# A three-pass fp32 feed-forward whose split weight sums are stored by the first token group and loaded by the other two

## The chip, the cores and the metric

The kernel runs on one core of one Trainium2 chip. A core has TensorE (PE in the profile), VectorE (DVE), ScalarE (ACT), GpSimd (POOL), and SyncE (SP), which in this kernel issues nearly all DMA transfers; each engine executes its own instruction list in order. The metric is the device time of one execution in microseconds (us). The kernel before takes 2158.03 us, the median of three runs (2157.86 to 2159.79).

## The reference

One layer of a decoder in fp32, over 2048 prompt tokens and 8 sample tokens, model width 1024, feed-forward width 2816:

```python
def _layer(x, ...):
    xn = _rmsnorm(x, norm1_g)
    z = jnp.einsum('btd,de->bte', xn, w_in)        # [xr | gr | q | k | v]
    ...                                            # RG-LRU group, windowed attention group
    mix = jnp.concatenate([_rmsnorm(rec, rec_norm_g), _rmsnorm(att, attn_norm_g)], axis=-1)
    h = x + jnp.einsum('bte,ed->btd', mix, w_out)
    hn = _rmsnorm(h, norm2_g)
    ff = jax.nn.silu(jnp.einsum('btd,df->btf', hn, w_gate)) * jnp.einsum('btd,df->btf', hn, w_up)
    y = h + jnp.einsum('btf,fd->btd', ff, w_down)
    return y, new_k, new_v, new_conv, h_last
```

A last RMSNorm gives the outputs; the caches and recurrent states are outputs too.

## The kernel before

**Two phases.** Phase A (to about 706 us) computes the norm, the input projection, the RG-LRU and attention groups and the output projection, for four sub-sequences of some 512 tokens. The residual stream h goes to the DRAM tensor `hs`. Phase B is the feed-forward. It goes over three token groups (0, 1, 2), each of two halves of 344 or 342 columns, and in each group over 11 pairs of 128-row chunks of the feed-forward width.

**Three passes per product.** A matrix product in fp32 is made of three passes of a reduced-precision format (fp32r): each operand is split into a high part (the cast) and a low part (value minus cast), and TensorE adds high x high, high x low and low x high.

**Seven products per pair.** Gate and up are computed by a scheme of the Strassen kind (Winograd's variant): a 2 x 2 block product needs seven block products in place of eight, of sums of weight blocks and sums of token blocks. So per pair and matrix TensorE does 7 products of 12 matmuls, in the order `PRODS = [1, 2, 6, 7, 5, 3, 4]`, and then 96 plain matmuls for down. In its list g of pair p, down of pair p-1 and u of pair p follow each other.

**Weights.** `mixed_weights` (L995 of the kernel before) loads the four raw blocks of a pair and matrix, 256 KB each, from SyncE (L1000), and forms the sums S5, S6, S7 (`combine`, L1006; on GpSimd) and S3 (on VectorE). `keep_weights` then makes the split tile of each of the seven: the cast on ScalarE (L990) and the subtraction on GpSimd for products at even places of `PRODS`, on VectorE for odd ones (L991). A split tile is 512 KB, both parts side by side. `down_weights` (L1022) does the same without sums, all low parts on GpSimd. There are 7 buffers for raw blocks and 8 for split tiles. The same work is done in each of the three groups, from the same weights.

**Results.** `products` adds the seven PSUM results into c_g and c_u on VectorE (L1057), applies silu on ScalarE (L1048), multiplies (L1051), and splits the product into fh (cast, L1053) and fl (subtraction, L1054). `down` multiplies them (L1107 to L1109) and adds into y (L1111, VectorE). `finish` does the last norm and stores `out_yT` from SyncE (L1138); `y_load` (L986) reloads h into the buffers that come free.

**Tokens.** `hn_mix` reloads h from `hs` (n<-hs, L320), scales it (L324), forms the sums of token blocks (L332) and stores them in `mixed` (L328); `hn_load` loads them and splits them (L379 to L381).

**Order.** Every piece of work is a generator that yields due times (`Chains`); the due time becomes the priority of the instructions made next. A scheduler that simulates a timeline takes these priorities and fixes the order of each engine's list. So a change of due times or a removed instruction moves others. An engine that waits for a semaphore holds everything behind it in its list, SyncE's transfers included.

**The last sub-sequence.** While `out_half` finishes the last sub-sequence, ScalarE squares each of the eight chunks of h (L245, L248) and GpSimd adds seven of them into `hacc` (L249). `last_norm`, due at T_H3 = T_B0 + 25, makes the norm's factors of it.

## Time and profile before

| what | value |
|---|---|
| median of three runs | 2158.03 us (2157.86 to 2159.79) |
| the profiled execution | 2159.32 us, span 2157.5 us |
| TensorE busy | 2064.9 us (96%) |
| VectorE busy | 1504.3 us (70%) |
| ScalarE busy | 937.9 us (43%) |
| GpSimd busy | 1167.4 us (54%) |
| DMA | 300.73 MB, mean 139 GB/s |

"Busy" of TensorE includes modelled ends, so a full row doesn't mean peak speed. The trace gives for each instruction its start, its duration and, in brackets, the idle time before it and what ended it ("<-ACT w_g L990": it waited for the cast of line 990). Line numbers are those of the kernel before; in the kernel after, lines behind the first part of the diff have other numbers.

### The profile page before, as it was taken

To read this page: it belongs to the slowest core of one execution; us is meant where nothing else is said; L and a number is where in the kernel's file an instruction comes from. 1 tells how busy PE (TensorE), PEld (TensorE's weight loads), DVE (VectorE), ACT (ScalarE), POOL (GpSimd) and SP (SyncE) were. 2 spreads that over 40 slices of the span, in tenths; PEclk is the share of its full clock that TensorE was granted. 3 is DMA by queue.
4 is the path that set the end of the run, shared out by engine and by line. 5 is a ranking of instruction groups with operands and counts; after the bars stand their busy time and mean duration, and the time that the engine had idled before them with its cause. 6 is when DMAs were issued, how large, how long until landed. Compare 5 with 4: busy or idle time off the path is not lost.

```text
span 2157.5 us, 34673 instructions
## 1 busy us (share of the span) xinstructions
PE 2064.9 (96%) x12454; PEld 1950.7 (90%) x12454; DVE 1504.3 (70%) x2683; ACT 937.9 (43%) x1890; POOL 1167.4 (54%) x968
## 2 busy tenths in 40 slices
PE   8999899999999899999998999999998999999997
PEld 8887687878777799999998999999998999999997
DVE  6757974766985867766657867666758875565566
ACT  5746763563553533333334433333334433333332
POOL 5211342020122786676577866776677766765763
PEclk9999899999999999999999999999999999999999
DMA  8764384575677533333225242333225242222221
GB/s 304 244 211 137 126 295 152 176 256 192 208 248 268 165 108 97 100 111 109 92 73 175 81 158 90 100 123 105 93 75 168 87 136 74 84 79 74 69 79 53
DMA packets 155563, 300.73 MB, mean 139 GB/s; under 512 B 19424, under 2 KB 60784, under 8 KB 155376
## 3 DMA queue, kind: packets, MB, share of 16 engines
q1 hardware_dynamic: 152192, 296.00, 42.1%
q10 hardware_dynamic: 3200, 2.51, 0.4%
...
HBM read 243.62 MB, written 55.90 MB: 139 GB/s over the span
## 4 chain that ended last, share of the span: by engine, by line
PE 68%; DVE 12%; DMA 7%; POOL 4%; ACT 4%; issue 4%; SPq 1%; DVEq 0%; ACTq 0%; POOLq 0%
PE pd L1108 6%; PE pd L1109 6%; PE pd L1107 6%; PE ps_u L1067 6%; PE ps_u L1069 6%; PE ps_u L1068 6%; PE ps_g L1067 5%; PE ps_g L1069 5%; PE ps_g L1068 5%; PE ip L232 3%; PE ip L233 3%; PE ip L234 3%; DMA n<-hs 2%; PE op L233 1%; PE op L234 1%
## 5 line engine op out<-in xcount | busy, mean ns | idle before, releaser
L1107 PE MATMUL pd<-fh,w_d 128*128 128x342 f32 (+1 forms) x1056 | 339.4, 323 | 12.2 <-DVE y L1111 6.6
L1108 PE MATMUL pd<-fl,w_d 128*128 128x342 f32 (+1 forms) x1056 | 340.7, 323 | 9.7 <-DVE fl L1054 9.7
L1109 PE MATMUL pd<-fh,w_d 128*128 128x342 f32 (+1 forms) x1056 | 340.4, 323 | 0.0
L1067 PE MATMUL ps_g<-hn,w_g 128*128 128x342 f32 (+1 forms) x924 | 296.0, 321 | 7.8 <-ACT w_g L990 6.1
L1111 DVE TENSOR_TENSOR y<-y,pd 128x342 f32<-128x342 f32 (+1 forms) x528 | 249.5, 503 | 71.5 <-PE pd L1109 68.8
L1067 PE MATMUL ps_u<-hn,w_u 128*128 128x342 f32 (+1 forms) x924 | 295.4, 320 | 1.9 <-DVE y L1111 1.6
L1069 PE MATMUL ps_g<-hn,w_g 128*128 128x342 f32 (+1 forms) x924 | 296.0, 320 | 0.0
L1068 PE MATMUL ps_g<-hn,w_g 128*128 128x342 f32 (+1 forms) x924 | 295.8, 320 | 0.0
L1068 PE MATMUL ps_u<-hn,w_u 128*128 128x342 f32 (+1 forms) x924 | 295.0, 319 | 0.0
L1069 PE MATMUL ps_u<-hn,w_u 128*128 128x342 f32 (+1 forms) x924 | 294.9, 320 | 0.0
L1107 PEld LDWEIGHTS pd<-fh,w_d 128*128 128x128 f32 x1056 | 200.2, 190 | 16.9 <-DVE y L1111 8.0
L232 PE MATMUL ip<-xn,w_in 128*128 128x512 f32 (+1 forms) x560 | 199.6, 364 | 13.2 <-ACT xn L237 9.2
L1108 PEld LDWEIGHTS pd<-fl,w_d 128*128 128x128 f32 x1056 | 201.8, 191 | 10.4 <-DVE fl L1054 10.4
L233 PE MATMUL ip<-xn,w_in 128*128 128x512 f32 (+1 forms) x560 | 201.6, 364 | 0.5 <-DVE xn L238 0.5
L1109 PEld LDWEIGHTS pd<-fh,w_d 128*128 128x128 f32 x1056 | 201.8, 191 | 0.0
L234 PE MATMUL ip<-xn,w_in 128*128 128x512 f32 (+1 forms) x560 | 199.0, 358 | 0.2 <-POOL w_in L223 0.2
L991 POOL TENSOR_TENSOR w_d<-rd,w_d 128x512 fp32r<-128x512 f32 x132 | 182.9, 1396 | 1.5 <-ACT w_d L990 1.3
L1067 PEld LDWEIGHTS ps_g<-hn,w_g 128*128 128x128 f32 x924 | 174.8, 189 | 8.4 <-ACT w_g L990 6.4
L991 POOL TENSOR_TENSOR w_u<-ru,w_u 128x512 fp32r<-128x512 f32 x66 | 98.7, 1495 | 152.5 <-ACT w_u L990 152.5
L1057 DVE TENSOR_TENSOR c_u<-c_u,ps_u 128x342 f32<-128x342 f32 (+1 forms) x231 | 114.3, 507 | 92.4 <-PE ps_u L1069 90.8
L1067 PEld LDWEIGHTS ps_u<-hn,w_u 128*128 128x128 f32 x924 | 174.1, 188 | 2.7 <-ACT w_g L990 1.4
L1069 PEld LDWEIGHTS ps_g<-hn,w_g 128*128 128x128 f32 x924 | 174.8, 189 | 0.2 <-DVE w_g L991 0.2
...
## 6 DMA issues: line engine op xcount, KB each, us to landing
w_in<-split_w SPq DMA_DIRECT2D x84, 512.0 KB, 3.5
...
w_out<-split_w SPq DMA_DIRECT2D x48, 512.0 KB, 5.0
split_w<-w_in SPq DMA_DIRECT2D x28, 512.0 KB, 5.1
...
```

What stands on the lines that cost most here:

```text
L232: nc.tensor.matmul(out, wh, xh, start=first, stop=False)
L233: nc.tensor.matmul(out, wh, xl, start=False, stop=False)
L234: nc.tensor.matmul(out, wl, xh, start=False, stop=last)
L991: lo_eng.tensor_tensor(w[:, 1, :], src, w[:, 0, :].bitcast(F32), op=ALU.subtract)
L1057: nc.vector.tensor_tensor(o, a, b, op)
L1067: nc.tensor.matmul(ps, wh, hi, start=kk == 0, stop=False)
L1068: nc.tensor.matmul(ps, wh, lo, start=False, stop=False)
L1069: nc.tensor.matmul(ps, wl, hi, start=False, stop=kk == 3)
L1107: nc.tensor.matmul(ps, w[:, 0, c:c + P], hi, start=h == 0, stop=False)
L1108: nc.tensor.matmul(ps, w[:, 0, c:c + P], lo, start=False, stop=False)
L1109: nc.tensor.matmul(ps, w[:, 1, c:c + P], hi, start=False, stop=h == 1)
L1111: nc.vector.tensor_tensor(ys[gi, n, m], ys[gi, n, m], ps, ALU.add)
```

## The change

In group 0, the split tiles of products 6, 7, 5 and 3 are also stored, each 512 KB, from SyncE to a DRAM tensor for gate or up (L_ST = 5 before the product's due time; 2 after it for the first pair). In groups 1 and 2 these four tiles are loaded from there (L_SS = 11 before the product's due time), the raw block A21 is not loaded, and its sums, casts and subtractions are not made. Products 1, 2 and 4 are split as before in every group.

The squares of the last sub-sequence no longer are made in `out_half`. `last_norm` reloads the eight chunks from `hs` (SyncE), due from T_B0 + 38 in steps of 4, squares them on ScalarE, adds them on GpSimd, and makes the norm's factors 6 after the last.

```diff
@@ -41,6 +41,7 @@
 DVE_MUL = 2
 N_EARLY = 3
 T_FS = 12.0
+L_SS, L_ST = 11.0, 5.0
 D_TB = 0.0
 U_M = 1.76
 U_G, U_D = 7 * U_M, 14.1
@@ -49,7 +50,7 @@
 T_OP = [187.9747, 327.9525, 449.1331, 501.2336]
 T_OPA, L_LM = 539.4805, 52.6622
 T_B0 = 586.0461
-T_H3 = T_B0 + 25
+T_H3, D_H3 = T_B0 + 38, 4.0
 T_B = [T_B0 + i * (NPAIR * U_P + D_TB) for i in range(3)]
 O_KF = [8, 9, 10, 11, 12, 13, 0, 4, 1, 5, 2, 6, 3, 7]
 O_KL = [0, 4, 1, 5, 2, 6, 3, 7, 8, 9, 10, 11, 12, 13]
@@ -195,6 +196,7 @@
         rs2 = cp.tile([P, 4, 5], F32, name="rs2")
         hs = dp.tile([P, KD, NTOK], F32, name="hs")
         mixed = dp.tile([3, 7, P, 4, TP], F32, name="mixed")
+        split_s = {x: dp.tile([NPAIR, 4, P, 2, 512], F32, name=f"split_{x}") for x in "gu"}
         split_w = dp.tile([22, 2, P, 2, 512], F32, name="split_w")
 
         warm = cp.tile([P, 1], F32, name="warm")
@@ -885,13 +887,7 @@
                 with ahead(L_EV):
                     nc.vector.tensor_tensor(ps[:, :T], ps[:, :T], state[s]["late"][:, :T], ALU.mult)
                     nc.vector.tensor_tensor(xs[:, :T], xs[:, :T], ps[:, :T], ALU.add)
-                yield t + 3, ("hq", s, m - 1)
-                if m == 0:
-                    state[s]["hacc"] = accp.tile([P, TM], F32, tag="acc", name=f"hacc{s}")
-                acc = state[s]["hacc"]
-                add_square(acc, xs[:, :T], T, m == 0, f"h{s}_{m}")
                 nc.scalar.dma_start(hs[:, m, c0:c0 + T], xs[:, :T])
-                fire(("hq", s, m))
 
             def fin_a():
                 yield (T_OP[2], ("h", 3, 3), ("xr", 3, 3), ("h", 3, 2), ("h", 3, 1), ("h", 3, 0))
@@ -991,11 +987,17 @@
                 lo_eng.tensor_tensor(w[:, 1, :], src, w[:, 0, :].bitcast(F32), op=ALU.subtract)
                 ws[key] = w
                 fire(key)
+                return w
+
+            SPLIT = (6, 7, 5, 3)
 
             def mixed_weights(src, gi, p, x):
                 yield t_prod(gi, p, x, 0) - 18
                 A = {}
                 for h, q in ((0, 0), (0, 1), (1, 0), (1, 1)):
+                    if gi and (h, q) == (1, 0):
+                        A[h, q] = None
+                        continue
                     A[h, q] = raw_tile(f"r{x}{gi}_{p}_{h}{q}")
                     nc.sync.dma_start(A[h, q], src[2 * p + h][:, q * 512:q * 512 + 512])
                 A11, A12, A21, A22 = A[0, 0], A[0, 1], A[1, 0], A[1, 1]
@@ -1008,16 +1010,27 @@
 
                 S = {1: A11, 2: A12, 4: A22}
                 for i, r in enumerate(PRODS):
-                    yield t_prod(gi, p, x, i) - 9
+                    tr = t_prod(gi, p, x, i)
+                    if gi and r in SPLIT:
+                        yield tr - L_SS
+                        w = whl_tile(f"w_{x}{gi}_{p}_{r}")
+                        nc.sync.dma_start(w.bitcast(F32), split_s[x][p, SPLIT.index(r)])
+                        ws[x, gi, p, r] = w
+                        fire((x, gi, p, r))
+                        continue
+                    yield tr - 9
                     if r == 6:
                         S[5] = combine(A21, A22, ALU.add, 1)
                         S[6] = combine(S[5], A11, ALU.subtract, 2)
-                        yield t_prod(gi, p, x, i) - 8
+                        yield tr - 8
                     if r == 7:
                         S[7] = combine(A11, A21, ALU.subtract, 3)
                     if r == 3:
                         S[3] = combine(A12, S[6], ALU.subtract, 4)
-                    keep_weights((x, gi, p, r), f"{x}{gi}_{p}_{r}", S[r], nc.gpsimd if i in LO_POOL else nc.vector)
+                    w = keep_weights((x, gi, p, r), f"{x}{gi}_{p}_{r}", S[r], nc.gpsimd if i in LO_POOL else nc.vector)
+                    if r in SPLIT:
+                        with at(tr - L_ST if p else tr + 2):
+                            nc.sync.dma_start(split_s[x][p, SPLIT.index(r)], w.bitcast(F32))
 
             def down_weights(gi, p, t):
                 for i, (q, h) in enumerate(((0, 0), (0, 1), (1, 0), (1, 1))):
@@ -1138,9 +1151,20 @@
                     nc.sync.dma_start(yT[:, m, o:o + nn], v)
 
             def last_norm(s):
-                _, T, _, w, nt = SUBS[s]
-                yield T_H3
-                rstd_cols(state[s]["hacc"][:, :T], w, nt, 0, rs2[:w, s, :nt], f"h{s}", 0, True)
+                c0, T, _, w, nt = SUBS[s]
+                for m in range(KD):
+                    yield T_H3 + D_H3 * m
+                    if m == 0:
+                        acc = accp.tile([P, TM], F32, tag="acc", name=f"hacc{s}")
+                    x = stage(f"h{s}_{m}")[:, :T]
+                    keep(nc.sync.dma_start(x, hs[:, m, c0:c0 + T]))
+                    if m == 0:
+                        nc.scalar.square(acc[:, :T], x)
+                    else:
+                        nc.scalar.square(x, x)
+                        nc.gpsimd.tensor_tensor(acc[:, :T], acc[:, :T], x, op=ALU.add)
+                yield T_H3 + D_H3 * KD + 6
+                rstd_cols(acc[:, :T], w, nt, 0, rs2[:w, s, :nt], f"h{s}", 0, True)
                 fire(("h", s))
 
             ch.add(last_norm(3))
```

The instruction lists of before and after differ at many places; three of them matter below. In the names, `w_g_0_6` is the split gate tile of pair 0 and product 6, `s_g_0` a sum of gate blocks of pair 0, `rg_4_00` a raw block, `fl_10_10` a low part of pair 10; the number behind the last underscore is that of the allocation.

GpSimd, passage from phase A to phase B; before:

```order
L991 TENSOR_TENSOR w_g_0_5_7763<-s_g_0_7751,w_g_0_5_7763 128x512
L991 TENSOR_TENSOR w_g_0_6_7755<-s_g_0_7753,w_g_0_6_7755 128x512
L249 TENSOR_TENSOR hacc_6969<-hacc_6969,sq_h_1_6989 128x512
L249 TENSOR_TENSOR hacc_6969<-hacc_6969,sq_h_2_7010 128x512
L249 TENSOR_TENSOR hacc_6969<-hacc_6969,sq_h_3_7031 128x512
L249 TENSOR_TENSOR hacc_6969<-hacc_6969,sq_h_4_7050 128x512
L249 TENSOR_TENSOR hacc_6969<-hacc_6969,sq_h_5_7069 128x512
L249 TENSOR_TENSOR hacc_6969<-hacc_6969,sq_h_6_7088 128x512
L249 TENSOR_TENSOR hacc_6969<-hacc_6969,sq_h_7_7094 128x512
L1006 TENSOR_TENSOR s_g_0_7758<-rg_0_00_7664,rg_0_10_7668 128x512
L991 TENSOR_TENSOR w_g_0_4_7785<-rg_0_11_7670,w_g_0_4_7785 128x512
```

and now:

```order
L987 TENSOR_TENSOR w_g_0_1_7716<-rg_0_00_7643,w_g_0_1_7716 128x512
L1008 TENSOR_TENSOR s_g_0_7738<-rg_0_00_7643,rg_0_10_7647 128x512
L1008 TENSOR_TENSOR s_g_0_7730<-rg_0_10_7647,rg_0_11_7649 128x512
L1008 TENSOR_TENSOR s_g_0_7732<-s_g_0_7730,rg_0_00_7643 128x512
L987 TENSOR_TENSOR w_g_0_5_7744<-s_g_0_7730,w_g_0_5_7744 128x512
L987 TENSOR_TENSOR w_g_0_6_7734<-s_g_0_7732,w_g_0_6_7734 128x512
L1008 TENSOR_TENSOR s_u_0_7828<-ru_0_10_7726,ru_0_11_7728 128x512
L987 TENSOR_TENSOR w_u_0_1_7786<-ru_0_00_7722,w_u_0_1_7786 128x512
L1008 TENSOR_TENSOR s_u_0_7830<-s_u_0_7828,ru_0_00_7722 128x512
L1008 TENSOR_TENSOR s_u_0_7852<-ru_0_00_7722,ru_0_10_7726 128x512
```

The seven adds are gone from here, the third gate sum stands first, and the sums for the up matrix follow directly.

VectorE, end of group 0 (pair 10) and beginning of group 1 (pair 0); before:

```order
L381 TENSOR_TENSOR hn_1_4_12588<-hn_1_4_12588 128x342
L1051 TENSOR_TENSOR c_u_10_10_7300<-c_u_10_10_7300,c_g_10_10_7288 128x344
L991 TENSOR_TENSOR w_g_0_7_12756<-s_g_0_12754,w_g_0_7_12756 128x512
L1054 TENSOR_TENSOR fl_10_01_7295<-c_u_10_01_7299,fh_10_01_7291 128x344
L381 TENSOR_TENSOR hn_1_5_12609<-hn_1_5_12609 128x342
L381 TENSOR_TENSOR hn_1_7_12620<-hn_1_7_12620,hn_1_6_12616 128x342
L1057 TENSOR_TENSOR c_g_0_00_7302<-c_g_0_01_7303,ps_g_0_2_12657 128x342
L1054 TENSOR_TENSOR fl_10_10_7296<-c_u_10_10_7300,fh_10_10_7292 128x344
```

and now:

```order
L1070 TENSOR_TENSOR c_u_10_10_7279<-c_u_10_10_7279,ps_u_10_4_12684 128x344
L383 TENSOR_TENSOR hn_1_3_12673<-hn_1_3_12673,hn_1_2_12669 128x342
L1064 TENSOR_TENSOR c_u_10_10_7279<-c_u_10_10_7279,c_g_10_10_7267 128x344
L1067 TENSOR_TENSOR fl_10_01_7274<-c_u_10_01_7278,fh_10_01_7270 128x344
L383 TENSOR_TENSOR hn_1_4_12680<-hn_1_4_12680 128x342
L383 TENSOR_TENSOR hn_1_5_12701<-hn_1_5_12701 128x342
L1067 TENSOR_TENSOR fl_10_10_7275<-c_u_10_10_7279,fh_10_10_7271 128x344
L1070 TENSOR_TENSOR c_g_0_00_7281<-c_g_0_01_7282,ps_g_0_2_12749 128x342
```

The weight subtraction, one token split and the add into c_g no longer stand ahead of `fl_10_10`; `hn_1_4` now does.

TensorE at the same place, shortly ahead of that fl; before (ahead of these rows stand nine down matmuls of the first three outputs with the 00 parts):

```order
L1107 MATMUL pd_10_3_0_12722<-fh_10_00_7290,w_d_10_00_12555 128x344
L1108 MATMUL pd_10_3_0_12722<-fl_10_00_7294,w_d_10_00_12555 128x344
L1109 MATMUL pd_10_3_0_12722<-fh_10_00_7290,w_d_10_00_12555 128x344
L1107 MATMUL pd_10_4_0_12738<-fh_10_00_7290,w_d_10_01_12676 128x344
L1108 MATMUL pd_10_4_0_12738<-fl_10_00_7294,w_d_10_01_12676 128x344
L1107 MATMUL pd_10_0_0_12695<-fh_10_10_7292,w_d_10_10_12624 128x344
L1107 MATMUL pd_10_1_0_12703<-fh_10_10_7292,w_d_10_10_12624 128x344
L1107 MATMUL pd_10_2_0_12714<-fh_10_10_7292,w_d_10_10_12624 128x344
L1107 MATMUL pd_10_3_0_12722<-fh_10_10_7292,w_d_10_10_12624 128x344
L1108 MATMUL pd_10_0_0_12695<-fl_10_10_7296,w_d_10_10_12624 128x344
```

and now, from the first down matmul on:

```order
L1120 MATMUL pd_10_0_0_12787<-fh_10_00_7269,w_d_10_00_12647 128x344
L1121 MATMUL pd_10_0_0_12787<-fl_10_00_7273,w_d_10_00_12647 128x344
L1122 MATMUL pd_10_0_0_12787<-fh_10_00_7269,w_d_10_00_12647 128x344
L1120 MATMUL pd_10_0_0_12787<-fh_10_10_7271,w_d_10_10_12716 128x344
L1120 MATMUL pd_10_1_0_12795<-fh_10_00_7269,w_d_10_00_12647 128x344
L1121 MATMUL pd_10_1_0_12795<-fl_10_00_7273,w_d_10_00_12647 128x344
L1122 MATMUL pd_10_1_0_12795<-fh_10_00_7269,w_d_10_00_12647 128x344
L1121 MATMUL pd_10_0_0_12787<-fl_10_10_7275,w_d_10_10_12716 128x344
L1122 MATMUL pd_10_0_0_12787<-fh_10_10_7271,w_d_10_10_12716 128x344
```

The first matmul with `fl_10_10` was the 19th of the down matmuls and is now the 8th.

SyncE in a steady stretch of group 1, pairs 3 and 4; before:

```order
L1000 DMA rg_4_00_14336<-in_wgate 128x512
L1000 DMA rg_4_01_14338<-in_wgate 128x512
L1000 DMA rg_4_10_14340<-in_wgate 128x512
L1026 DMA rd_3_10_14595<-in_wdown 128x512
L1000 DMA rg_4_11_14342<-in_wgate 128x512
L320 DMA n_4_0_14426<-hs 128x342
L1026 DMA rd_3_00_14516<-in_wdown 128x512
L328 DMA mixed<-n_4_0_14426 128x342
L328 DMA mixed<-n_0_1_13837 128x342
L320 DMA n_1_1_14611<-hs 128x342
L1000 DMA ru_4_01_14651<-in_wup 128x512
L1026 DMA rd_3_01_14631<-in_wdown 128x512
```

and now:

```order
L1002 DMA rg_4_00_14339<-in_wgate 128x512
L1002 DMA rg_4_01_14341<-in_wgate 128x512
L1002 DMA rg_4_11_14343<-in_wgate 128x512
L1002 DMA ru_4_00_14622<-in_wup 128x512
L1039 DMA rd_3_00_14495<-in_wdown 128x512
L1039 DMA rd_3_10_14568<-in_wdown 128x512
L1017 DMA w_u_3_6_14319<-split_u 128x1024
L1017 DMA w_u_3_7_14337<-split_u 128x1024
L1017 DMA w_u_3_5_14361<-split_u 128x1024
L1017 DMA w_u_3_3_14379<-split_u 128x1024
L322 DMA n_4_0_14411<-hs 128x342
L330 DMA mixed<-n_4_0_14411 128x342
```

One raw load less stands there, and four loads of split up tiles stand behind the raw loads of the next pair.

## The prediction

> **What bounds the kernel now.** I read three views in this order: the windows by stage, the groups and waits of TensorE, and then, around each gap, the instructions in order of time. All times are microseconds of the profiled execution (span 2157.5, its own time 2159.32). The median of the three timed runs is 2158.03, so 1.3 is taken off at the end.
>
> ```profile
> 706.00:745.00 39.00, 29.77 (x170) 28.04 (x169) 36.46 (x44) 21.12 (x43) 31.40 (x22) 0.91 0.55 177
> 745.00:1150.00 405.00, 401.30 (x2544) 399.60 (x2544) 271.05 (x442) 146.18 (x279) 285.40 (x222) 1.00 0.31 100
> 1150.00:1320.00 170.00, 158.56 (x988) 156.14 (x987) 133.08 (x199) 70.43 (x147) 122.09 (x94) 0.96 0.40 129
> 1320.00:1640.00 320.00, 319.06 (x2024) 318.02 (x2023) 215.56 (x350) 113.38 (x215) 217.33 (x169) 1.00 0.31 98
> 1640.00:1760.00 120.00, 108.97 (x675) 106.88 (x675) 101.82 (x142) 54.24 (x115) 92.61 (x74) 0.96 0.46 148
> 1760.00:2140.00 380.00, 380.00 (x2413) 380.00 (x2413) 229.62 (x391) 134.93 (x256) 242.57 (x194) 1.00 0.22 70
> ```
>
> In the window rows stand start and end, length, busy time of PE, PEld, DVE, ACT and POOL, then granted clock, DMA share and GB/s. The feed-forward phase starts near 706. Its long stretches are full: from 1760 to 2140 TensorE is busy 380.00 of 380.00. A matmul starts every 380.00 / 2413 = 0.157. No work taken off another engine gains anything there. What is not full: 9.2 us at the passage from phase A (706 to 745), 3.7 in group 0, 11.4 and 11.0 around the two changes of token group, 0.9 in group 1. That is 36 us, and the clock rows below 1.00 add a little: after a long idle the matmuls run slowly for some microseconds.
>
> ```profile
> 726.67 0.65 PE L1067 MATMUL ps_g<-hn,w_g 128*128 128x344 f32 x1 [6.09 <-ACT w_g L990]
> 1180.82 0.97 PE L1107 MATMUL pd<-fh,w_d 128*128 128x344 f32 x4 [1.75 <-ACT fh L1053]
> 1186.54 0.65 PE L1108 MATMUL pd<-fl,w_d 128*128 128x344 f32 x1 [4.75 <-DVE fl L1054]
> 1186.99 0.49 PE L1109 MATMUL pd<-fh,w_d 128*128 128x344 f32 x1
> 1187.28 0.49 PE L1108 MATMUL pd<-fl,w_d 128*128 128x344 f32 x1
> 1661.89 0.75 PE L1107 MATMUL pd<-fh,w_d 128*128 128x342 f32 x3 [2.72 <-ACT fh L1053]
> 1667.96 0.65 PE L1108 MATMUL pd<-fl,w_d 128*128 128x342 f32 x1 [4.95 <-DVE fl L1054]
> ```
>
> The number in brackets is the idle time before the row. These three places hold most of the loss. The granted clock counts as well: right after 4.75 of idle the matmuls start 1187.28 - 1186.99 = 0.29 apart, against 0.157. That lasts for some 17 matmuls by my count, 17 x 0.13 = 2.2 us, behind each of the long idles (6.09, 4.75, 4.95); the whole that could be won is 36 + 3 x 2.2, some 43 us, with smaller slow stretches perhaps 50. **The Trainium skill**, TensorE: Matmul & The Clock Gate, Part 1 (What's actually happening), says that the array goes to half its clock after an idle window of about 3.4 us and needs about as long to come back; the rows agree in kind, and by it a stall shortened below that window would also lose its slow tail.
>
> **The change, part by part.** First, the squares of the last sub-sequence. Eight squares on ScalarE and seven adds on GpSimd leave the passage.
>
> ```profile
> 711.64 7.20 POOL L249 TENSOR_TENSOR hacc<-hacc,sq_h 128x512 f32<-128x512 f32 x5
> 723.03 1.54 POOL L1006 TENSOR_TENSOR s_g<-rg,rg 128x512 f32<-128x512 f32 x1
> L381 DVE TENSOR_TENSOR hn<-m,hn 128x344 fp32r<-128x344 f32 x15 | 16.0, 1092 | 1.9 <-ACT hn L380 1.9
> 725.89 0.50 DVE L381 TENSOR_TENSOR hn<-m,hn 128x344 fp32r<-128x344 f32 x1
> 726.00 0.62 ACT L990 CAST w_g<-s_g 128x512 fp32r<-128x512 f32 x1 [2.83 <-DVE s_g L1006]
> ```
>
> Five adds take 7.20 of GpSimd, so the seven 10.1, and the third sum of the first gate weights stands behind them: it starts at 723.03, and VectorE's sum, the cast at 726.00 and TensorE follow. In the new order all three sums stand ahead, and TensorE first does other products (two of the up matrix). So the 6.09 wait loses the GpSimd part of its cause. But VectorE is busy 36.46 of the 39 there, and nothing is taken from it in group 0; it sets the end now as before. It is faster only where GpSimd was beside it: the 15 hn operations take 1.09 in the mean, some 0.50 where GpSimd rests (the row at 725.89). If that excess, 16.0 - 15 x 0.50 = 8.5, falls with GpSimd's load (10.1 of 31.40), it is 2.7 us. Low end of the gain 2 (VectorE's chain decides), high end 11 (all idle but what waits for the output projection, with the slow spell). I take **5**, nearer to the low end because VectorE is nearly full. The reload brings eight loads of 256 KB and puts the squares (8 x 0.61 by a cast of that size, below: 5) and the adds into pairs 0 and 1. From 745 to 1150 GpSimd is busy 285 of 405 and ScalarE 146, and nothing in group 0 waits for the result: nothing is charged. Were that cover gone, it would cost the 10.1.
>
> Second, group 0 stores 88 tiles of 512 KB, 46 MB, from SyncE's queue.
>
> ```profile
> w_in<-split_w SPq DMA_DIRECT2D x84, 512.0 KB, 3.5
> w_out<-split_w SPq DMA_DIRECT2D x48, 512.0 KB, 5.0
> split_w<-w_in SPq DMA_DIRECT2D x28, 512.0 KB, 5.1
> DVE n L324 <- DMA n<-hs: 55.1, 34, 3.9
> PE pd L1107 <- DVE y L1111: 2.5, 3, 1.7
> ```
>
> Like stores in phase A land in 5.1. The 46 MB over the group's 490 us are 94 GB/s beside the 100 of the window, so the DMA share of 0.31 would come to about 0.6: there is room. What may suffer is small: VectorE waits for reloaded tokens (55.1 us in 34 waits over the whole run), and three such delays reach TensorE through y in group 0. Bounds: 3 gained (those waits change by luck) to 6 lost; I take **1 lost**.
>
> Third, groups 1 and 2 load these four of seven weights. Per pair this takes off 8 ScalarE casts, 10 GpSimd and 6 VectorE operations and two 256 KB loads, and adds eight loads of 512 KB.
>
> ```profile
> L990 ACT CAST w_u<-s_u 128x512 fp32r<-128x512 f32 x36 | 21.3, 614 | 53.5 <-PE pd L1109 53.4
> L991 POOL TENSOR_TENSOR w_u<-s_u,w_u 128x512 fp32r<-128x512 f32 x18 | 24.0, 1333 | 21.8 <-ACT w_u L990 21.8
> L991 DVE TENSOR_TENSOR w_u<-s_u,w_u 128x512 fp32r<-128x512 f32 x18 | 18.7, 1041 | 4.7 <-ACT w_u L990 4.7
> ```
>
> With these durations (from 1760 to 2140) for sums and subtractions alike, that is per pair 8 x 0.61 = 5 us of ScalarE, 10 x 1.33 = 13 of GpSimd and 6 x 1.04 = 6.2 of VectorE; over 22 pairs 110, 290 and 137 us. In the steady stretches TensorE covers all of it, so it is worth **0** there; I give 0.5 for the 0.9 idle in group 1.
>
> At the two changes of group it is on the path:
>
> ```profile
> 1178.30 0.81 DVE L381 TENSOR_TENSOR hn<-hn 128x342 fp32r<-128x342 f32 x1
> ...
> 1180.18 1.39 DVE L991 TENSOR_TENSOR w_g<-s_g,w_g 128x512 fp32r<-128x512 f32 x1
> 1181.49 1.58 DVE L1054 TENSOR_TENSOR fl<-c_u,fh 128x344 fp32r<-128x344 f32 x1
> 1182.99 1.22 DVE L381 TENSOR_TENSOR hn<-hn 128x342 fp32r<-128x342 f32 x1
> 1184.13 1.21 DVE L381 TENSOR_TENSOR hn<-hn,hn 128x342 fp32r<-128x342 f32 x1
> 1185.27 0.50 DVE L1057 TENSOR_TENSOR c_g<-c_g,ps_g 128x342 f32<-128x342 f32 x1
> 1185.69 0.80 DVE L1054 TENSOR_TENSOR fl<-c_u,fh 128x344 fp32r<-128x344 f32 x1
> 1172.00:1190.00 18.00, 11.50 (x60) 10.62 (x59) 18.00 (x19) 9.04 (x22) 18.00 (x15) 0.76 0.60 193
> ```
>
> VectorE is full for all 18 us. Between the product L1051 and the fl at 1185.69 that TensorE needs stand the weight subtraction (1.39), fl, two hn (1.22, 1.21) and an add (0.50). In the new order the subtraction, one hn and the add are gone from there, but one hn that stood ahead (0.81) has come in: 1.39 + 1.21 + 0.50 - 0.81 = 2.3 earlier. Against this TensorE's new order has only 7 of the 96 down matmuls ahead of the first that needs this fl, where it had 18: 11 x 0.157 = 1.7 of work now comes after it. The rest of the gain is what GpSimd, also full with 18.00, no longer holds up. Low end 0, high end 5; I take **2** for each change, **4** together.
>
> Behind the changes:
>
> ```profile
> PE pd L1107 <- DVE y L1111: 3.0, 3, 1.5
> 1240.65 1.12 PE L270 MATMUL bc_f<-cs,cols_f 86*128 86x86 f32 x8 [0.91 <-POOL cols_f L260]
> 1722.07 0.92 PE L270 MATMUL bc_f<-cs,cols_f 114*128 114x114 f32 x6 [1.83 <-POOL cols_f L260]
> 1244.59 4.80 SPq L1138 DMA_DIRECT2D out_yT<-y  x8
> ```
>
> The first row is the waits between 1236 and 1300 with VectorE late; with 6.2 of its work gone in each pair, most of that goes. Both waits for cols_f stand behind GpSimd's queue, which is 13 us per pair lighter. That is 3.0 + 0.91 + 1.83, and the windows (11.44 and 11.03, less the 6.5 and the 2.72 + 4.95 at the changes themselves) leave 4.9 and 3.4, with slow clock some 9: low end 0, high end 9, and I take **6**. The last row is SyncE's work there, which returns in rival B.
>
> Sum: 5 - 1 + 0.5 + 4 + 6 = 14.5. From 2159.3 that is 2144.8; less 1.3, **2143**.
>
> **The Trainium skill**, SBUF — State Buffer, section SBUF: two separate sides, has a rule that bears on the size: a VectorE operation with two SBUF inputs and a GpSimd operation that reads SBUF lock each other out whole. The hn row above (1.09 in the mean, 0.50 alone) agrees. Taken to its end it says that each GpSimd operation gone takes a wait from VectorE too, which is rival C.
>
> **The rivals.** A: the work was hidden and the chains of VectorE at the three places hold. For it: VectorE full in both rows (36.46 of 39; 18.00 of 18), and fewer matmuls ahead of the late fl. Against it: the seven adds really stand ahead of the sum that the 6.09 waited for. Then only 2 at the passage: 2158 - 2 = 2156, within 0.2%. This is also what a change without effect would give.
>
> B, on the other side: SyncE's in-order queue. A weight load is put 11 us ahead of its product, lands after 3.5 to 5.0, and so bears a hold-up of 6 to 7.5. It stands behind raw loads that wait for a buffer:
>
> ```profile
> SPq L1000 <- POOL w_g L991: 122.6, 21, 12.9
> ```
>
> These are the 21 waits of a raw load of gate or up in group 1 (1200 to 1680), the longest 12.9. In the new order four up-weight loads stand behind three gate loads and two down loads of the next pair. Where a 12.9 wait falls there, TensorE waits up to 6; with 1 in each of the 22 pairs of groups 1 and 2, 22 in all, less 8 of the gains that stay, the time is 2172. After a change of group three up-weight loads also stand behind the eight finished outputs of the row above, 4.80 of SyncE's time, and ten reloads. Against it: those waits were for buffers held by the GpSimd subtractions now gone, and each matrix takes 3 of the raw buffers, not 4. It decides from hold-ups over about 7.
>
> C: all three places lose their stalls because VectorE runs freely. 11 at the passage, 10 at the changes, 9 behind, 1 in group 1: 31, which gives 2127. For it: 1.09 against 0.50. Against it: GpSimd still does the hn splits at the changes of group, and the seven adds only were a third of its load at the passage.
>
> **How the numbers follow.** Forecast 0.52 (2130 to 2153), C 0.18, A 0.14, B 0.16. This measurement can tell about 0.2%, 4.3 us, from no change, so faster is 0.70, same 0.14, slower 0.16. The range goes down to 2122 (C's 2127 with the group 0 term at its gaining end, 4 better, and one more for the tail of C) and up to 2163, so that A is in it and B with little of C is left out, about 0.2; the likeliest case's own range is the 2130 to 2153.
>
> **What would show it.** Right: the gap near 726 shrinks to under 3 with the weight sums on GpSimd ahead of 715; VectorE still full there; the fl waits near 1187 and 1668 shorter by 1 to 3; the waits for y near 1290 gone; the windows of the steady stretches at 99% or more as before; DMA share near 0.6 in group 0. Wrong: a row of TensorE waiting for a DMA into w_g or w_u (B); the passage not shorter (A); idle in group 0 over 10 us, which would mean that the stores hold SyncE up.

## The result, and the profile after

The changed kernel takes 2135.82 us (median; runs from 2133.11 to 2140.20) against 2158.42 for the kernel before in the same comparison: ratio 0.9896, interval [0.9879, 0.9914]. That is 22.6 us faster. The profiled execution took 2133.11 (span 2131.3), so its trace shows 26.2 us less span than the one before, some 4 more than the medians.

Windows of the kernel after, cut where its stages now lie (start and end, length, PE, PEld, DVE, ACT, POOL, granted clock, DMA share, GB/s):

```profile
706.00:755.00 49.00, 45.31 (x268) 42.95 (x268) 42.12 (x54) 22.88 (x46) 32.01 (x24) 0.97 0.85 301
755.00:1150.00 395.00, 392.50 (x2489) 391.26 (x2490) 274.75 (x439) 143.27 (x275) 280.49 (x216) 1.00 0.58 203
1150.00:1300.00 150.00, 145.53 (x929) 144.67 (x928) 93.24 (x164) 53.78 (x114) 68.84 (x59) 0.99 0.69 229
1300.00:1610.00 310.00, 310.00 (x1971) 310.00 (x1970) 163.30 (x300) 78.81 (x156) 113.30 (x92) 1.00 0.58 188
1610.00:1730.00 120.00, 115.81 (x725) 115.24 (x724) 77.60 (x137) 45.87 (x97) 57.78 (x50) 0.97 0.70 233
1730.00:2114.00 384.00, 384.00 (x2439) 384.00 (x2438) 177.91 (x344) 96.66 (x191) 134.31 (x112) 1.00 0.46 151
```

Group 0 now moves 203 GB/s in place of 100, at a DMA share of 0.58. The idle of TensorE around the changes of group fell from 11.4 and 11.0 to 4.5 and 4.2. In the steady stretch of group 2, GpSimd is busy 134 of 384, before 243 of 380, and VectorE 178 against 230. TensorE is full there as it was.

What TensorE waited for from 706 on in the kernel before, the five longest rows (total, times, longest):

```profile
PE pd L1108 <- DVE fl L1054: 9.7, 2, 5.0
PE pd L1107 <- DVE y L1111: 6.6, 9, 1.7
PE ps_g L1067 <- ACT w_g L990: 6.1, 1, 6.1
PE pd L1107 <- ACT fh L1053: 4.5, 2, 2.7
PE bc_f L270 <- POOL cols_f L260: 3.2, 3, 1.8
```

and what it still waits for there in the kernel after, the six longest of eleven:

```profile
PE pd L1121 <- DVE fl L1067: 4.3, 2, 2.4
PE pd L1120 <- ACT fh L1066: 3.9, 2, 2.3
PE ps_g L1081 <- DVE hn L383: 2.4, 2, 1.7
PE op L234 <- DVE xres L889: 2.2, 1, 2.2
PE st_f L257 <- DVE acc_f L251: 1.8, 1, 1.8
PE pd L1120 <- DVE y L1124: 1.0, 2, 0.6
```

None of the eleven rows has a DMA into w_g or w_u. The wait of 6.1 for a cast of w_g is gone, the waits for fl fell from 9.7 to 4.3, those for y from 6.6 to 1.0. At the passage the first sums of gate weights now start at 702 and their subtractions end before 710; VectorE's token splits are what TensorE waits for:

```profile
702.46 2.79 POOL L1008 TENSOR_TENSOR s_g<-rg,rg 128x512 f32<-128x512 f32 x2 [5.59 <-DMA rg<-in_wgate]
732.83 0.42 PE L1081 MATMUL ps_g<-hn,w_g 128*128 128x344 f32 x1 [1.74 <-DVE hn L383]
```

**Where the time went.** TensorE executes the same matmuls in both kernels, so the last of each pair's 96 down matmuls (its start) is a mark that both traces have. I cut the feed-forward at these marks: P, the passage, runs from the first gate matmul to pair 1's mark; G0 to pair 9 of group 0; change 1 from there to pair 1 of group 1; and so on. The tail runs from the last down matmul to the end. The table is worked out from the TensorE instructions of each trace, in us:

| kernel | P | G0 | change 1 | G1 | change 2 | rest of G2 | tail | span |
|---|---|---|---|---|---|---|---|---|
| before | 109.6 | 336.9 | 146.7 | 334.2 | 142.5 | 361.2 | 15.5 | 2157.5 |
| after | 106.1 | 333.3 | 136.1 | 332.4 | 134.6 | 361.2 | 17.0 | 2131.3 |
| reload alone | 113.7 | 335.8 | 147.6 | 334.2 | 141.9 | 361.2 | 16.6 | 2165.8 |
| split tiles alone | 114.8 | 332.3 | 134.7 | 332.4 | 134.5 | 361.2 | 15.5 | 2133.8 |
| stores, no loads | 107.9 | 332.3 | 144.4 | 335.9 | 142.1 | 361.2 | 16.8 | 2154.1 |
| loads due 6 ahead | 107.5 | 332.3 | 133.5 | 332.4 | 134.7 | 361.2 | 15.4 | 2132.8 |
| idle sums on GpSimd | 109.2 | 332.3 | 143.7 | 332.4 | 143.6 | 361.2 | 15.6 | 2151.5 |
| idle sums on VectorE | 109.7 | 332.3 | 134.1 | 332.5 | 134.6 | 361.2 | 15.6 | 2132.6 |
| idle fills on GpSimd | 107.9 | 332.3 | 137.3 | 332.4 | 134.8 | 360.8 | 15.9 | 2132.2 |
| products 7 and 3 only | 109.0 | 332.3 | 139.6 | 332.4 | 141.6 | 360.8 | 15.5 | 2141.9 |
| fewer buffers | 115.9 | 334.3 | 137.4 | 345.3 | 141.1 | 362.6 | 15.6 | 2163.2 |
| all seven products | 114.4 | 333.4 | 133.8 | 332.4 | 133.2 | 361.2 | 16.7 | 2131.8 |
| four and down | 105.9 | 333.1 | 133.4 | 332.1 | 132.0 | 360.8 | 16.6 | 2123.9 |
| all seven and down | 112.9 | 332.4 | 131.2 | 332.4 | 132.6 | 361.2 | 15.6 | 2126.9 |

The changed kernel gains 18.5 at the two changes of group (10.6 and 7.9), 3.5 at the passage, 3.6 in group 0 and 1.8 in group 1, and loses 1.5 in the tail. Up to the first gate matmul TensorE's list is the same in all fourteen, yet that matmul starts between 706.8 and 715.9. A span or a single time therefore tells less than the table, and medians of kernels differ by what this spread leaves in them: the kernel before ran from 2146.9 to 2162.6 in the comparisons below. Each row of the table is one trace, too. The kernel with loads due 6 ahead has the same list on TensorE as the changed kernel throughout, and still takes 133.5 at change 1 where that takes 136.1; so differences below some 3 us in one column are not told apart.

### The profile page after: what moved, and what is told of

It is laid out like the page before. It is cut to its first block, busy times and chain, and to the rows that moved or that the text cites. A ratio compares the mean times of both kernels' runs of the same rounds, so it can differ in the third digit from the quotient of the medians.

```text
span 2131.3 us, 34656 instructions
## 1 busy us (share of the span) xinstructions
PE 2057.4 (97%) x12454; PEld 1947.2 (91%) x12454; DVE 1346.7 (63%) x2551; ACT 838.2 (39%) x1714; POOL 863.4 (41%) x748
## 4 chain that ended last, share of the span: by engine, by line
PE 74%; DVE 10%; DMA 8%; ACT 3%; issue 3%; POOL 1%; SPq 0%; DVEq 0%; ACTq 0%; POOLq 0%
PE pd L1120 7%; PE pd L1121 7%; PE pd L1122 7%; PE ps_u L1082 6%; PE ps_u L1080 6%; PE ps_u L1081 6%; PE ps_g L1082 6%; PE ps_g L1081 6%; PE ps_g L1080 6%; PE ip L234 3%; PE ip L235 3%; PE ip L236 3%; DMA n<-hs 2%; DMA xs<-in_xT 1%; PE op L235 1%
## 5 line engine op out<-in xcount | busy, mean ns | idle before, releaser
L1124 DVE TENSOR_TENSOR y<-y,pd 128x342 f32<-128x342 f32 (+1 forms) x528 | 259.9, 508 | 152.4 <-PE pd L1122 142.0
L987 POOL TENSOR_TENSOR w_u<-ru,w_u 128x512 fp32r<-128x512 f32 x66 | 90.9, 1377 | 439.6 <-ACT w_u L986 436.6
L986 ACT CAST w_u<-ru 128x512 fp32r<-128x512 f32 x99 | 60.8, 620 | 372.5 <-PE pd L1122 245.2
L1064 POOL TENSOR_TENSOR c_u<-c_u,c_g 128x342 f32<-128x342 f32 (+1 forms) x120 | 124.0, 1035 | 168.3 <-DVE c_u L1070 167.2
L1070 DVE TENSOR_TENSOR c_g<-c_g,ps_g 128x342 f32<-128x342 f32 (+1 forms) x231 | 113.4, 506 | 103.7 <-PE ps_g L1082 102.1
```

Source lines behind the costliest of these rows:

```text
L987: lo_eng.tensor_tensor(w[:, 1, :], src, w[:, 0, :].bitcast(F32), op=ALU.subtract)
L1070: nc.vector.tensor_tensor(o, a, b, op)
L1124: nc.vector.tensor_tensor(ys[gi, n, m], ys[gi, n, m], ps, ALU.add)
```

## The experiments

**Each part alone.** Two kernels have one of the two parts each. The first is the kernel before with the new `last_norm` and without the squares in `out_half`; the second is the kernel after with the old ones:

```diff
 # the second kernel, against the kernel after
+                yield t + 3, ("hq", s, m - 1)
...
+                add_square(acc, xs[:, :T], T, m == 0, f"h{s}_{m}")
                 nc.scalar.dma_start(hs[:, m, c0:c0 + T], xs[:, :T])
+                fire(("hq", s, m))
```

> The kernel before with only the second part of the change: the squares of the last sub-sequence from a reload; no stores and no loads of split tiles. Theory (the two parts add, and this one pays only at the passage): the first gate sums stand ahead on GpSimd, the 6.1 us wait near 726 goes, the first pair takes 4 to 5 us less (it took 67.4 before, 63.1 after the whole change), everything from the second pair on within 1 us of before: about 2154. Rival 1 (the passage gained because the stores made the scheduler choose another order): the first pair takes 66 or more, time 2157 to 2159. Rival 2 (VectorE, freed of waits for GpSimd, runs ahead and the later d-phase stalls of group 0 go too): 2150 or less.

> The whole change without its second part: stores and loads of the split tiles, the squares still made while the last sub-sequence finishes. Theory (parts add): first pair as before, some 67 us, all of the gain at the two changes of token group and in groups 0 and 1: 22.6 less some 4.5, so 18 us below before, about 2140. Rival 1 (the stores need the freed passage, SyncE held up by adds on GpSimd): first pair over 69, time 2143 or more. Rival 2 (the passage gains anyway by another order): 2136 or less.

Measured: the reload alone 2158.66, ratio 1.0018 [1.0002, 1.0035]; the split tiles alone 2137.29, ratio 0.9918 [0.9902, 0.9934]. What TensorE waits for from 700 to 830 in the kernel with the reload alone:

```profile
PE pd L1101 <- ACT c_g L1066: 3.1, 1, 3.1
PE op L232 <- DVE xres L887: 2.1, 1, 2.1
PE pd L1101 <- DVE rs L259: 2.0, 1, 2.0
PE ps_g L1062 <- DVE hn L381: 2.0, 4, 0.9
```

and from 700 to 780 in the kernel with the split tiles alone (in both, the longest rows):

```profile
PE ps_g L1086 <- ACT w_g L992: 6.9, 1, 6.9
PE ps_g L1086 <- DVE xres L889: 1.6, 1, 1.6
```

GpSimd, ahead of that wait in the second kernel, has five of the adds and behind them the third gate sum:

```profile
710.38 7.56 POOL L251 TENSOR_TENSOR hacc<-hacc,sq_h 128x512 f32<-128x512 f32 x5
722.35 1.26 POOL L1014 TENSOR_TENSOR s_g<-rg,rg 128x512 f32<-128x512 f32 x1
```

So the mechanism was right: where the seven adds stand in the passage, TensorE waits 6.9 for the cast of w_g behind them, and where they are gone that wait is gone. But what I expected of it was not: without the stores the scheduler writes another order, in which the place of the wait is taken by one of 3.1 for c_g, 2.0 for the norm's factors (which now come from the reload) and several for hn. The reload alone gains nothing by its median; its P of 113.7 against 109.6 comes from the slowest of its twelve executions (2167.54). In these traces the parts do not add: each alone has a longer P than before, both together a shorter one. All of the gain at the changes of group comes from the split tiles (134.7 and 134.5).

Why the two parts fit together at the passage is a matter of the scheduler's order, which differs in all three on every engine; no run isolates it. Six of the profiled kernels (the changed one, the stores without loads, the loads due 6 ahead and the three with idle work) have the same instruction lists on TensorE and VectorE up to about 1135, near the end of group 0. Their P runs from 106.1 to 109.7, mean 108.1. So the 3.5 of the changed kernel's trace is the upper end of what the passage gives; 1.5 is its mean, and against the one trace of the kernel before (109.6) even that is not clear of the spread.

**Stores without loads.** Groups 1 and 2 make all tiles themselves:

```diff
-                    if gi and (h, q) == (1, 0):
+                    if False:
...
-                    if gi and r in SPLIT:
+                    if False:
...
-                    if r in SPLIT:
+                    if r in SPLIT and gi == 0:
```

> The whole change, but groups 1 and 2 make all seven split tiles themselves as before; the stores of group 0 stay, nobody reads them. Theory: the stores ride along free, DMA share of group 0 about 0.58 as after the change, group 0 as fast as after the change (pairs 1 to 9 some 3 us less than before), the two changes of group as before: about 2151, 7 below before. Rival 1 (stores cost, and the changed trace hides it behind gains from elsewhere): 2156 or more. Rival 2 (the gain at the first change of group comes from group 0's order, not from the loads): 2145 or less.

Measured: 2153.18, ratio 0.9986 [0.9974, 0.9997]. Group 0 (755 to 1150) in this kernel:

```profile
755.00:1150.00 395.00, 392.74 (x2498) 391.75 (x2497) 273.42 (x437) 145.90 (x282) 289.76 (x222) 1.00 0.57 202
```

The 46 MB of stores are free: DMA share 0.57, and G0 is 332.3, 4.6 less than before. Where those 4.6 lie can be read: in the pairs in which TensorE waited for y before. There VectorE had waited up to 3.9 for a token reload (n<-hs) with the y additions behind it:

```profile
1020.55 1.43 DVE L324 SCALAR_TENSOR_TENSOR n<-n,vec,hb 128x342 f32<-128x342 f32 x1 [3.85 <-DMA n<-hs]
1025.76 1.34 DVE L1111 TENSOR_TENSOR y<-y,pd 128x344 f32<-128x344 f32 x3
```

In the new order no reload is waited for at that place. That is a matter of order and not of the stores' own work: the reload alone, which has another order, has only 1.1 of it. The changes of group stay at 144.4 and 142.1. They gain by the loads.

**Due time of the loads.** Only L_SS is 6.0 in place of 11.0.

> The whole change with the loads of split tiles put 6 us ahead of their products instead of 11. The loads land after 4.2 to 4.5 us. Theory (they are free as long as they bear a hold-up of some us; 6 leaves about 1.5): TensorE now waits for a DMA into w_g or w_u in many pairs, at 0.5 to 1 us each over 22 pairs 10 to 20 us: 2146 to 2156. Rival (the order on SyncE leaves the loads early enough anyway, since the due time only sets their place among other transfers): within 3 us of the changed kernel, 2133 to 2139.

Measured: 2132.92, ratio 0.9892 [0.9878, 0.9907]. The rival was right: no wait for a DMA into w_g or w_u, times as in the changed kernel. From the issues on SyncE and the matmuls that first use each tile, the lead of the 176 loads is 7.8 to 25.9 us, median 14.6, in the changed kernel, and 7.8 to 26.7, median 13.8, here. A load lands after 4.2 to 4.5 (medians). So the due time does not set the lead. The shortest lead (7.8) is that of `w_u_1_7`, behind the finished outputs after a change of group, the place that the prediction named.

**Fewer buffers.** What could set the lead is the number of tile buffers:

```diff
-                return (wp if turn("whl", 8) < 5 else wp2).tile(...
+                return (wp if turn("whl", 4) < 1 else wp2).tile(...
```

> The whole change with three in four split tiles turning over 3 buffers and the fourth over 5, in place of 8 buffers for all. With 8 buffers the loads are issued 7.8 to 26 us (median 14.6) ahead of the first matmul that uses them, whatever their due time: 7 and 6 tiles of about 2.3 us each give 14 to 16. Theory (the buffers, not the due times, set the lead of a load; the rival on the slower side of the prediction decides from there): a depth of four gives a lead of some 3 x 2.3 = 7, and 4.3 us of landing still fit, so waits for a DMA appear only here and there: 5 to 20 us slower than the changed kernel. Rival (the leads do not come from the buffers): leads stay above 10 and the time within 3 us.

Measured: 2165.03, ratio 1.0038 [1.0025, 1.0051], 29 above the changed kernel's median. Leads are now 4.0 and more, median 6.0. TensorE, from 1150 to 2120:

```profile
PE ps_g L1080 <- DMA w_g<-split_g: 8.9, 6, 2.4
PE ps_u L1080 <- DMA w_u<-split_u: 4.6, 3, 3.3
PE pd L1120 <- DVE c_g L1070: 3.7, 2, 3.2
```

13.5 us of waits for the loads themselves, in nine places. So the buffers do set the lead, and the prediction's rival B exists, but with eight buffers it is a margin of 3 us away. The loss was above the 20 expected; some of it is not the loads': the tiles that are still made on the engines have fewer buffers too, and P is 115.9.

**Which engine's relief pays.** Two kernels leave the loads as they are and give one engine back idle work in groups 1 and 2: as many sums as the change took from it.

```diff
+                    if gi and r in SPLIT:
+                        def idle_op(eng):
+                            ...
+                            eng.tensor_tensor(v[:, :512], A11, A22, op=ALU.add)
+                        with at(tr - 9):
+                            for _ in range({6: 3, 7: 1, 5: 1, 3: 0}[r]):   # the other kernel: {6: 0, 7: 1, 5: 0, 3: 2}
+                                idle_op(nc.gpsimd)                         # and nc.vector
```

> The whole change, but in groups 1 and 2 GpSimd makes ten sums per pair (of two raw blocks, due 9 us ahead of the product) that nobody reads, as many as the change took from it; VectorE and ScalarE stay relieved. Theory (the changes of group pay because VectorE's chain there is shorter, and VectorE is slowed by GpSimd beside it, so both reliefs share it): the pairs around the two changes, 10.7 and 7.9 us better in the changed kernel, keep 40 to 60% of that, the time comes out 7 to 11 us above the changed kernel. Rival 1 (VectorE's own relief pays, GpSimd's not): within 3 us of the changed kernel. Rival 2 (GpSimd's relief pays all): 16 us or more above it.

> The whole change, but in groups 1 and 2 VectorE makes six sums per pair that nobody reads, as many as the change took from it; GpSimd and ScalarE stay relieved. Theory: the other half of the gain at the changes of group goes, 7 to 11 us above the changed kernel. Rival 1 (VectorE's own relief pays all): 16 us or more above it. Rival 2 (GpSimd's relief pays): within 3 us of it.

Measured: with GpSimd's idle sums 2150.24, ratio 0.9964 [0.9953, 0.9976]; with VectorE's 2136.40, ratio 0.9909 [0.9888, 0.9930]. My theory, a half each, falls: VectorE takes its six operations per pair back at no cost (changes of group 134.1 and 134.6), while GpSimd's ten bring them to 143.7 and 143.6, in total nearly as long as before. One place at the first change shows how. First VectorE, then GpSimd, then TensorE of the kernel with idle sums on GpSimd (start, duration, instruction, idle before):

```profile
1236.32 6.89 DVE L987 TENSOR_TENSOR w_u<-ru,w_u 128x512 fp32r<-128x512 f32 x1
1243.14 0.50 DVE L1078 TENSOR_TENSOR c_g<-c_g,ps_g 128x342 f32<-128x342 f32 x1
```

```profile
1236.50 2.50 POOL L1018 TENSOR_TENSOR x_u<-ru,ru 128x512 f32<-128x512 f32 x2
1238.97 3.69 POOL L1018 TENSOR_TENSOR x_g<-rg,rg 128x512 f32<-128x512 f32 x3
```

```profile
1243.69 0.65 PE L1128 MATMUL pd<-fh,w_d 128*128 128x342 f32 x1 [4.24 <-DVE c_g L1078]
```

A subtraction that takes 0.68 alone lasts 6.89, until the fifth of five GpSimd sums in a row has ended; the add behind it is late, and TensorE stands 4.24. The add itself, which reads PSUM and only one SBUF tile, takes its usual 0.50. **The Trainium skill** states this as a lock (SBUF — State Buffer, section SBUF: two separate sides): a VectorE operation with two SBUF inputs and a GpSimd operation that reads SBUF exclude each other for the whole instruction. The trace agrees, and goes further: here the loser was passed over by five instructions in a row.

At the second change the longest wait, 4.25 for a y, has another shape:

```profile
1715.55 7.88 DVE L1156 SCALAR_TENSOR_TENSOR y<-y,vec,rb_f 128x342 f32<-128x342 f32 x8 [1.53 <-ACT rb_f L278]
1725.46 0.65 PE L1128 MATMUL pd<-fh,w_d 128*128 128x342 f32 x1 [4.25 <-DVE y L1132]
```

The first four of the eight scalings alternate with GpSimd's sums and take 1.37 to 1.60 each, the last four, with no sum beside them, 0.56. The 1.53 ahead of them goes back to cols_f on GpSimd, which stands 1.3 behind an idle sum: that part is GpSimd's own list being late.

But these sums stand closer together than the real work did: the longest such subtraction in the kernel before lasts 1.8. Nor do they bring back the waits of the kernel before. The next table splits the two changes by pairs (pair 10 of the old group, pairs 0 and 1 of the new one) and gives the busy time of VectorE, with its instructions, and of GpSimd over the three; the last two runs are described below:

| kernel | change 1: pairs 10, 0, 1 | VectorE | GpSimd | change 2: pairs 10, 0, 1 | VectorE | GpSimd |
|---|---|---|---|---|---|---|
| before | 43.6, 56.9, 46.2 | 116.1 (169) | 109.3 | 44.5, 57.7, 40.3 | 117.0 (168) | 106.2 |
| after | 40.1, 55.7, 40.3 | 88.2 (153) | 62.8 | 41.4, 52.1, 41.1 | 84.3 (150) | 61.9 |
| idle sums on GpSimd | 38.3, 66.1, 39.3 | 99.0 (153) | 101.7 | 41.6, 60.4, 41.6 | 96.9 (150) | 102.2 |
| idle sums on VectorE | 37.1, 58.3, 38.7 | 98.1 (171) | 62.6 | 40.6, 52.4, 41.6 | 97.4 (168) | 61.6 |
| idle fills on GpSimd | 41.4, 57.8, 38.0 | 92.8 (151) | 129.0 | 40.9, 52.9, 41.0 | 85.2 (150) | 103.2 |
| products 7 and 3 only | 41.5, 59.0, 39.2 | 99.1 (153) | 95.9 | 43.1, 56.7, 41.8 | 95.6 (150) | 95.6 |

The idle sums lose their time in pair 0 alone; the kernel before lost it in pairs 10 and 1 at the first change and in pairs 10 and 0 at the second. And VectorE is as busy with its own idle sums as with GpSimd's beside it, yet only GpSimd's cost time: not the sum of VectorE's busy time decides, but which operation is held where. Nobody reads the idle sums, so only their due times place them. Two more kernels were run.

**Fills in place of sums.** The idle sums become fills that keep GpSimd busy and read nothing:

```diff
-                            eng.tensor_tensor(v[:, :512], A11, A22, op=ALU.add)
+                            eng.memset(v[:, :520], 0.0)
...
-                            for _ in range({6: 3, 7: 1, 5: 1, 3: 0}[r]):
+                            for _ in range({6: 8, 7: 2, 5: 3, 3: 0}[r]):
```

> As the run with idle sums on GpSimd, but each group of idle sums is a group of fills of 128x520 (8, 2 and 3 per matrix, estimated at 0.5 each from a fill of 64x640 in 0.63), which keep GpSimd busy about as long and write SBUF but do not read it. Theory (a GpSimd operation that reads SBUF blocks VectorE operations with two SBUF inputs; fills do not): VectorE's longest subtraction stays under 1.8, the waits of 4.2 and 4.3 behind VectorE are gone, time within 4 us of the changed kernel. Rival (it is GpSimd's own in-order list that is late): within 4 us of the run with idle sums, 2150.

Measured: 2134.23, ratio 0.9888 [0.9869, 0.9907]. Windows from 1165 to 1260, in this order: before, after, with idle sums on GpSimd, with fills.

```profile
1165.00:1260.00 95.00, 87.60 (x554) 86.38 (x553) 84.99 (x121) 44.23 (x95) 71.98 (x55) 0.95 0.47 155
```

```profile
1165.00:1260.00 95.00, 90.53 (x579) 89.67 (x578) 64.11 (x110) 34.20 (x73) 44.15 (x39) 0.98 0.71 239
```

```profile
1165.00:1260.00 95.00, 85.69 (x530) 84.05 (x529) 72.04 (x105) 32.65 (x74) 67.59 (x56) 0.95 0.63 218
```

```profile
1165.00:1260.00 95.00, 90.35 (x572) 89.50 (x571) 63.87 (x109) 33.70 (x73) 87.54 (x134) 0.96 0.69 238
```

With fills GpSimd is busy 87.54 of 95, more than in any other kernel, and the time is that of the changed one; VectorE is busy 63.87, as after (64.11), against 72.04 with the sums. The fixed window does not hold the same work in each kernel; between the marks (table above) VectorE is busy 92.8 at the first change with fills, against 88.2 after and 99.0 with sums. The fills wait for no raw block and so run ahead of their places: none between 1511 and 1697, none after 1788. But at both changes GpSimd is at least as busy with them as with the sums. So in the main it is not GpSimd's own list being late; it is what its SBUF reads do to VectorE. The order of the lists is the scheduler's own in each kernel and is not the same in both. The waits of 4.2 and 4.3 are gone, as expected; the waits for fl are 6.1 in all, 4.3 after. The longest subtraction w_u is 2.25 (expected under 1.8).

**Half of the products.** With SPLIT = (7, 3) VectorE loses the same six operations per pair as in the whole change, GpSimd two of ten and ScalarE four casts of eight; the raw block A21 is loaded again. This is real work at its real places:

> The whole change with only products 7 and 3 stored and loaded: VectorE loses the same operations as in the whole change (two subtractions and a sum per matrix), GpSimd only one of five. Theory (from the two runs with idle work: GpSimd's relief pays at the changes of group, VectorE's own nearly nothing): the pairs around the changes keep a quarter of the 10.7 and 7.9, time 2147 to 2152. Rival (the idle sums on GpSimd hurt because they stood back to back and held one subtraction of VectorE for 6.9 us; the real work would not): 2136 to 2142.

Measured: 2145.77, ratio 0.9944 [0.9927, 0.9961], between theory and rival. The changes of group take 139.6 and 141.6, together 281.2, where before took 289.2 and after 270.7. So 8 of the 18.5 come with VectorE's relief (and two of GpSimd's operations), 10.5 only when GpSimd's other eight go (and ScalarE's other four casts). Together with the idle sums on VectorE (268.7) this says that the two reliefs can stand in for each other in part, but GpSimd's is enough without VectorE's. That last point rests on the idle sums alone: no run takes real work from GpSimd only. Nor does any run give ScalarE its casts back, so its share stays open; it kept its relief in the kernel with GpSimd's idle sums, which lost nearly all of the gain.

**Further on the same way.** If GpSimd's reads are what costs, more of them can go. Three kernels: all seven products of gate and up stored and loaded; the four of the change and the four down tiles; all seven and down. For down:

```diff
             def down_weights(gi, p, t):
                 for i, (q, h) in enumerate(((0, 0), (0, 1), (1, 0), (1, 1))):
+                    if gi:
+                        yield t + U_D / 4 * i - L_SS
+                        w = whl_tile(f"w_d{gi}_{p}_{h}{q}")
+                        nc.sync.dma_start(w.bitcast(F32), split_s["d"][p, i])
+                        ...
+                        continue
...
+                    with at(t + U_D / 4 * i - L_ST):
+                        nc.sync.dma_start(split_s["d"][p, i], w.bitcast(F32))
```

> The whole change with all seven split tiles stored and loaded, no raw loads of gate and up in groups 1 and 2. 66 more stores and 132 more loads of 512 KB, 132 raw loads of 256 KB less. Theory (what is left around the changes of group is VectorE's token splits and fl, and TensorE is full elsewhere): 1 to 3 us below the changed kernel at the changes, nothing elsewhere, DMA share in group 1 about 0.75. Rival (the transfers are too many now: SyncE and the buffers hold the loads up): 5 us or more above it, with TensorE waiting for a DMA into w_g or w_u.

> The whole change, and the split down weights are stored by group 0 and loaded by groups 1 and 2 as well: 44 stores, 88 loads of 512 KB for 88 raw loads of 256 KB, and GpSimd loses its four down subtractions of 1.4 per pair, ScalarE four casts. Theory (GpSimd's relief pays at the changes): the waits for fh and fl at the changes, 1.6 + 2.4 and 2.3 + 1.9 with slow tails of about 2, shrink by 2 to 4 each: 2129 to 2133. Rival 1 (nothing left to win, VectorE's chain itself is the limit): within 2 us of the changed kernel. Rival 2 (too many transfers, as each buffer is now held by a load for some 14 us ahead): 3 us or more slower, with TensorE waiting for w_d from a DMA.

> All seven split tiles of gate and up and the four of down stored and loaded: GpSimd and ScalarE make no weights in groups 1 and 2, every pair loads 18 x 512 KB = 9.4 MB in 41.5 us, 227 GB/s beside the token reloads. Theory: GpSimd is free at the changes, 2 to 5 us below the changed kernel as long as the transfers hold; DMA share some 0.8 in group 1. Rival: the transfers do not hold, TensorE waits for w_d, w_g or w_u from a DMA, 10 us or more above it.

Measured: all seven 2135.08, ratio 0.9898 [0.9882, 0.9914]; four and down **2126.14, ratio 0.9846 [0.9830, 0.9862]**; all seven and down 2128.82, ratio 0.9860 [0.9841, 0.9879]. The changed kernel's interval, [0.9879, 0.9914], lies above that of four and down: this version has the lowest median of all, though the two were compared with the kernel before and not with each other, and its interval overlaps that of all seven and down. Three of TensorE's waits in it:

```profile
PE pd L1129 <- ACT fh L1075: 2.4, 1, 2.4
PE pd L1129 <- DMA w_d<-split_d: 2.0, 1, 2.0
PE pd L1130 <- DVE fl L1076: 0.9, 1, 0.9
```

The waits for fl fell from 4.3 to 0.9; a new one of 2.0 for a down tile's load has come. Its changes of group take 133.4 and 132.0, 5.3 less than after, and 2.8 less than with the loads due 6 ahead (133.5 and 134.7). Its DMA share in group 1 is 0.64:

```profile
1300.00:1610.00 310.00, 310.00 (x1973) 310.00 (x1972) 150.57 (x300) 60.52 (x121) 66.95 (x58) 1.00 0.64 215
```

With all seven and down the changes are no longer (131.2 and 132.6), and the passage has one of the bad orders (P 112.9), as with all seven alone (114.4). What the rival feared, that the transfers do not hold, is not seen: even at 252 GB/s in group 1 (DMA share 0.73, 0.8 expected) TensorE waits 2.9 for loads in all. Of the three expectations, 1 to 3 below the changed kernel for all seven came out as no difference, 2129 to 2133 for four and down as better than that, and 2 to 5 below for all seven and down as 7.

## Why the prediction was right, and where it was not

The forecast was 2143 with 2130 to 2153 for the likeliest case; measured 2135.8. Direction and places held. Of the mechanism, the order of the lists at the passage was right; at the changes of group the prediction priced VectorE's own shorter list, and what GpSimd no longer holds up was worth more. The size was a third too low, 14.5 against 22.6 by the medians. That the sum still fell into its range owes something to luck: group 0, booked as a loss, gained by an order that nobody had foreseen. Point by point:

- **The passage, 5.** The 6.09 wait went, as said, and VectorE's list is what TensorE now waits for there (hn, 2.4). 3.5 came in the trace of the changed kernel, 1.5 in the mean of six kernels with the same lists. The step that failed is that the reload brings this by itself: alone it is no faster than the kernel before, since the scheduler puts other waits in the place. Nor was the reloaded sum free: the second pair waits 1.0 for hacc.
- **Group 0, 1 lost.** The stores cost nothing, as argued from the DMA share (0.6 forecast, 0.58 measured). That the waits for y would go (3.6 gained, 4.6 in the other five) was named in the bound only as a change by luck.
- **Steady stretches, 0 and 0.5.** Right: group 2 is unchanged to 0.1; group 1 gained 1.8.
- **The changes of group and behind them, 4 and 6.** This is the term that was mis-sized: 10 was forecast and 18.5 came, 6.6 in the two pairs 10 (forecast 4) and 11.9 in the pairs behind them (forecast 6). The waits for fl themselves fell by 2.3 and 3.1, about as forecast. The step counted VectorE's own operations that went, by their durations, and left what GpSimd no longer holds up as a rest without a number. The runs show the reverse: the idle sums on VectorE cost nothing, those on GpSimd take as much as nearly all of the gain, if in other pairs, and with real work eight of GpSimd's ten operations (and four casts of ScalarE) make 10.5 of 18.5. VectorE's busy time over the two changes fell by 27.9 and 32.8 with 16 and 18 instructions fewer, about 1.8 an instruction, where 1.04 was counted: a part of its busy time had been waiting for GpSimd.
- **The slow tail.** The prediction said, by **the Trainium skill** (TensorE: Matmul & The Clock Gate, Part 1), that a stall shortened below some 3.4 would lose its slow tail. That did not hold here. After an idle of 2.43, with one of 1.59 and four matmuls ahead of it, the matmuls again start 0.29 apart:

```profile
1171.36 0.58 PE L1120 MATMUL pd<-fh,w_d 128*128 128x344 f32 x2 [1.59 <-ACT fh L1066]
1174.69 0.66 PE L1121 MATMUL pd<-fl,w_d 128*128 128x344 f32 x1 [2.43 <-DVE fl L1067]
1175.14 0.49 PE L1122 MATMUL pd<-fh,w_d 128*128 128x344 f32 x1
1175.43 0.49 PE L1120 MATMUL pd<-fh,w_d 128*128 128x344 f32 x1
```

  Two idles close together, neither of them near 3.4, were followed by the slow clock here. The tail is shorter at this place, 11 matmuls against 18 before; at the second change, behind idles of 2.30 and 1.88, it is 21 against 17. The fl at this place came 11.9 earlier in the trace (1174.69 against 1186.54), of which 7.4 had been gained before (pair 9's mark).
- **Rival A** (hidden) is out. **Rival B** was not near: leads of 7.8 and more where 4.5 are needed; the condition is the number of buffers and not the 11 of the due time, from which I worked. **Rival C** had the right mechanism for the changes of group: it gave them 19, and 18.5 came. Its 11 at the passage did not come. That four and down reaches 2126, about C's 2127, is by other terms (23.8 at the changes, 3.7 at the passage).
- **The tail** was not in the sum: 1.5 longer in the changed kernel, where the last twelve broadcasts run at the slow clock, and 0 to 1.3 in the others.
